# A two-layer hybrid decoder step on one core: squares at the layer seam in PSUM, the decode update of the linear attention ahead of its outputs, and operand sums as a pipeline

## The chip, the cores and the metric

The kernel runs on one core of one Trainium2 chip. The metric is the device time of one execution in microseconds (us), here the median of 3 runs. The core has five engines: TensorE (PE in the profile; PEld is its weight load), VectorE (DVE), ScalarE (ACT), GpSimd (POOL) and SyncE (SP, which issues DMAs). TensorE writes to PSUM, the other memory on the chip is SBUF.

## The reference

One inference step over 1024 prompt rows and 8 decode rows, 1024 channels, two layers. Layer 0 is a gated linear attention of 4 heads beside a short gated convolution; layer 1 a Conformer convolution of width 31; RMS norms stand ahead of each and at the end. Cut to what the change touches:

```
def trunk(x, ...):
    for layer in range(2):
        h = rmsnorm(x, norm_g[layer])           # mean of squares over the 1024 channels
        out = even_layer(h, ...) if layer % 2 == 0 else odd_layer(h, ...)
        x = x + out                             # the seam: x's squares feed the next rmsnorm
    return rmsnorm(x, final_norm_g)

# even_layer, per head; S is (128, 256), one for the prompt and one for each decode row
S_t = diag(a_t) S_{t-1} + k_t^T v_t             # state update
o_t = q_t S_t                                   # output
o   = rmsnorm(o, gla_norm_g) * silu(g)
y   = gate_b * dwconv3(gate_c * hb) * silu(z_b) # projections of h: hb, gate_b, gate_c, z_b
out = concatenate([o, y]) @ w_out
```

All is float32.

## The kernel before

Activations lie transposed: 128 channels on the partitions, 1032 columns (1024 prompt and 8 decode rows) along the free axis, in three blocks of 384, 384 and 264 columns (`CH`). Each product of float32 operands is made of three products of float32r parts: operands are split into a high part (a copy on ACT, `wh`, L240) and a low part (a subtraction, `wl`, L244, on POOL or DVE). A *unit* (L274, called from `units`) is 24 such matmuls, 8 channel tiles by 3 products, for one 128-channel output block and one block of columns, into one of four PSUM buffers of the pool `mmp`. Everything else that needs PSUM takes one of four buffers of the pool `gp` (`g_t`).

All small SBUF tiles come from one ring, `T(...)`, of 25 equal slots: `ring = tc.tile_pool(name="ring", bufs=25)`. A tile keeps its slot until its last reader is done; a new tile waits, with the instruction that writes it, until a slot comes free. The order of ACT's instructions is as written. The order on the other engines is laid down by a planner when the kernel is built, from its own estimates of readiness; at run time every engine works through its queue in order.

Side work is in generators that are called *jobs*: `tick()` runs each started job for one step, and every unit (and every tile of a V projection) ends with a tick. A job that yields n sits out the next n ticks.

Stages in order: V projections (`v_proj`, L351, nine tiles for a head, evacuated by DVE L354); per head the k and q units, `gla(h)` as a job beside `g_proj(h)` (six units) and the next V projection; then sixteen pairs of blocks for the short convolution, of which pairs 3 to 14 are made by a Strassen-like scheme of 7 products (`pair_products`, L728) from sums of operand blocks; the output projection (`x1_add`, L906); the seam (`x1_stat`, `x1_norm`, L884 to L887); layer 1; the final norm.

In `gla(h)` a job step each is: scores (L513); transposes, loads of the decode state and of a, k, q spread over the partitions (`abc`, `kbc`, `qbc`, L538); two steps of state sums (L552, L558); two steps of outputs (L570, L573 on PE, copy L574 on ACT); then the decode state update (POOL multiplies by a, L577; sixteen ACT copies `kv`, L580; POOL adds, L581; store L582); then the decode outputs (POOL product L586, DVE reduction L587), the squares (L590, L591), their sum (L592) and its split (`in_parts`: ACT L397, POOL L398). `OSQ_WAIT` = 4 ticks later the squares are summed over channels on PE (`colsum_parts`, L405), and the norm is applied (L598, L599); 4 ticks after that the result is split (ACT L602, POOL L603) and stored (L605, L606). The gates of the next head (`gates`, L458 to L488, with a scan on DVE, L468) are another job, started `HEAD_AT` = 6, 3, 1 ticks after `gla`.

`build_t` is a job that starts in the first pair, after 6 ticks. It makes the sums of x blocks for the seven products: for each quarter k two loads (L685), two scalings on ACT (L686), four subtractions on DVE (L691 to L694) and three splits (ACT L696, POOL L697). The third pair (q = 2) waits for it before its second block's last units; `pair_sums` (L254 to L257) and `first_pair` (L707, L708) follow there. In the third pair DVE evacuates PSUM at L803 and L801.

At the seam the ring holds the eight x1 tiles, `ss1` and the sixteen tiles of `Bm`, the parts of the short convolution's result that the output projection reads. The sums of the last output block (f = 7) lie in three `gp` buffers. `x1_stat(c)` makes the column sum (L392) and 1/rms; it is written into the middle of a unit of the next block of columns.

Of the kernel before, what the change touches and what calls it, by code (L numbers as in the profile page):

```python
# [7 lines left out]
F32 = mybir.dt.float32  # L8
F32R = mybir.dt.float32r
I32 = mybir.dt.int32  # L10
AF = mybir.ActivationFunctionType
ALU = mybir.AluOpType
# [3 lines left out]
P = 128  # L16
NP = 1024
ND = 8
NT = NP + ND
CH = [(0, 384), (384, 384), (768, 264)]  # L20
KT = 8
# [40 lines left out]
def hybrid_step(ctx, tc, xT, wv, wa, wup, woa, wic, woc, par, ident_d, mask_d, smask_d, sgla, ssc, scc,  # L62
                y_o, glap_o, scp_o, ccp_o, glas_o, scs_o, ccs_o):
    nc = tc.nc
    pe, act, dve, pool, sp = nc.tensor, nc.scalar, nc.vector, nc.gpsimd, nc.sync
# [12 lines left out]
    def nm(s):  # L78
        cnt[0] += 1
        return f"{s}{cnt[0]}"  # L80

    def T(shape, dt=F32, s="t"):
        return ring.tile(shape, dt, tag="t", name=nm(s))
# [4 lines left out]
    def g_t():  # L88
        return gp.tile([P, 512], F32, tag="g", name=nm("g"))
# [16 lines left out]
    def pcol(n, i):  # L106
        return prm[:, PAR[n] + i:PAR[n] + i + 1]
# [260 lines left out]
    vT = {}  # L368
# [133 lines left out]
    def gla(h, V):  # L502
# [33 lines left out]
        for j in (2, 1, 0):  # L536
            t = T([P, ND, P], s="bc")
            sp.dma_start(out=t, in_=dec_d[h, j].partition_broadcast(P))  # L538
            bc.append(t)
        abc, kbc, qbc = bc  # L540
        s0 = [T([P, ND, P], s="s0") for _ in range(2)]
# [5 lines left out]
        for Q in range(2):  # L547
            for jj in range(2):
# [4 lines left out]
                for j in range(2):  # L553
# [3 lines left out]
                    else:  # L557
                        dve.scalar_tensor_tensor(out=sv(p_), in0=sv(p_ - 1), scalar=sm[:, 24 + p_:25 + p_],  # L558
                                                 in1=ps[:, j * DV:(j + 1) * DV], op0=ALU.mult, op1=ALU.add)
            yield  # L560
        sp.dma_start(out=glap_o[h], in_=sv(7))
        o = [T([P, NT], s="o") for _ in range(2)]
        for Q in range(2):
            for hf in range(2):
                ps = g_t()
                hs = slice(hf * P, (hf + 1) * P)
                for j in range(4):
                    p_ = Q * 4 + j
                    lo = Q * 512 + j * P
                    pe.matmul(ps[:, j * P:(j + 1) * P], V[Q][:, j, hs], scT[:, Q, j * P:(j + 1) * P],  # L570
                              start=True, stop=(p_ == 0))
                    if p_ > 0:
                        pe.matmul(ps[:, j * P:(j + 1) * P], sv(p_ - 1)[:, hs], qe[:, lo:lo + P], start=False, stop=True)  # L573
                act.activation(o[hf][:, Q * 512:(Q + 1) * 512], ps, AF.Copy)  # L574
            yield
        for hf in range(2):
            pool.tensor_tensor(out=s0[hf], in0=s0[hf], in1=abc, op=ALU.mult)  # L577
            kv = T([P, ND, P], s="kv")
            for b in range(ND):
                act.activation(kv[:, b, :], kbc[:, b, :], AF.Copy, scale=vT[h][:, hf, b:b + 1])  # L580
            pool.tensor_tensor(out=s0[hf], in0=s0[hf], in1=kv, op=ALU.add)  # L581
            sp.dma_start(out=glas_o[h, hf], in_=s0[hf])  # L582
        yield
        pr = kbc
        for hf in range(2):
            pool.tensor_tensor(out=pr, in0=s0[hf], in1=qbc, op=ALU.mult)  # L586
            dve.tensor_reduce(out=o[hf][:, NP:], in_=pr, axis=mybir.AxisListType.X, op=ALU.add)  # L587
        sq = T([P, NT], s="osq")
        rso = T([P, NT], s="rso")
        act.activation(sq, o[0], AF.Square)  # L590
# [32 lines left out]
    for h in range(H):  # L623
        kq_proj(h)
        start(gla(h, Vs[h]))
        if h + 1 < H:
            start(gates(h + 1), HEAD_AT[h])
        g_proj(h)
        if h + 2 < H:
            Vs.append(v_proj(h + 2))  # L630
# [47 lines left out]
    TQ, T1 = {}, {}  # L678

    def build_t():  # L680
        n = CH[0][1]
        for k in range(4):
            a, b = T([P, 2 * n], s="xa"), T([P, 2 * n], s="xb")
            for t, kk in ((a, k), (b, k + 4)):
                sp.dma_start(out=t, in_=xT[:, kk, 0:2 * n])  # L685
                act.activation(t, t, AF.Copy, scale=pcol("g0", kk))  # L686
            ts = [T([P, 2, n], F32R, s="tq") for _ in range(3)]
            tf = T([P, 2 * n], s="tf")
            f = [tf[:, :n], tf[:, n:], b[:, :n]]
            yield  # L690
            dve.tensor_tensor(out=f[1], in0=b[:, n:], in1=a[:, n:], op=ALU.subtract)  # L691
            dve.tensor_tensor(out=a[:, n:], in0=a[:, n:], in1=a[:, :n], op=ALU.subtract)
            dve.tensor_tensor(out=f[0], in0=b[:, n:], in1=a[:, n:], op=ALU.subtract)
            dve.tensor_tensor(out=f[2], in0=b[:, :n], in1=f[0], op=ALU.subtract)  # L694
            for j in range(3):
                act.activation(ts[j][:, 0, :], f[j], AF.Copy)  # L696
                pool.tensor_tensor(out=ts[j][:, 1, :], in0=f[j], in1=ts[j][:, 0, :].bitcast(F32), op=ALU.subtract)  # L697
            for j in range(3):
                TQ[j + 2, k] = ts[j]
            T1[k] = a[:, n:]  # L700
            yield

    built = build_t()
    start(built, BUILD_AT)
    def first_pair():
# [153 lines left out]
    for lo, n in CH:  # L859
        s = slice(lo, lo + n)  # L860
# [41 lines left out]
    def x1_add(f, c, ps):  # L902
        lo, n = CH[c]
        s = slice(lo, lo + n)
        xt = x1[f]
        dve.tensor_tensor(out=xt[:, s], in0=ps, in1=xt[:, s], op=ALU.add)  # L906
        if f == 0:
            act.activation(ss1[:, s], xt[:, s], AF.Square)
        else:
            sq = g_t() if f < KT - 2 else T([P, 384], s="sq")  # L910
            act.activation(sq[:, :n], xt[:, s], AF.Square)
            dve.tensor_tensor(out=ss1[:, s], in0=sq[:, :n], in1=ss1[:, s], op=ALU.add)

    for f in range(KT - 2):
        x1_tile(f)
        sums = [None] * 3
        if f == 0:
            wy, wo = W("o", f, 1), W("o", f, 0, ahead=1)
            for ks in (slice(0, KT - 1), slice(KT - 1, KT)):
                for c in (0, 2, 1):  # L920
                    sums[c] = unit(c, y_terms(wy, c)[ks], into=sums[c], part=(True, False))
                    tick()
        else:
            wo = W("o", f, 0)
            for c in range(3):
                sums[c] = unit(c, a_terms(wo, O, c), part=(True, False))
                tick()
            wy = W("o", f, 1)
        for c in (0, 2, 1) if f == 0 else range(3):
            x1_add(f, c, unit(c, y_terms(wy, c) if f else a_terms(wo, O, c), into=sums[c]))  # L930
            tick()
        sp.dma_start(out=x1_d[f], in_=x1[f])
# [3 lines left out]
    fs = (KT - 2, KT - 1)  # L936
# [8 lines left out]
    for c, (lo, n) in enumerate(CH):  # L945
        for f in fs:
            if c == 0:
                wy[f] = W("o", f, 1, ahead=1)
            mid = (14, lambda c=c: x1_stat(c - 1)) if c and f == fs[0] else None
            x1_add(f, c, unit(c, y_terms(wy[f], c), mid, into=sums[f, c]))  # L950
            sp.dma_start(out=x1_d[f][:, lo:lo + n], in_=x1[f][:, lo:lo + n])
            if c:
                x1_norm(c - 1, range(4) if f == fs[0] else range(4, KT))
# [114 lines left out]
    for i in range(KT):  # L1068
# [28 lines left out]
        else:  # L1097
            for b, take in ((8 + i, take_gate), (i, take_u)):
                for c, s, ps in units(W("c", b), X):
# [4 lines left out]
                                 in1=pd[:, i, :], op0=ALU.mult, op1=ALU.add)  # L1104
# [237 lines left out]
```

## Time and profile before

| what | us |
|---|---|
| median of 3 runs (lowest, highest) | 1325.4 (1322.89, 1327.21) |
| the profiled execution | 1327.57 |
| its span, first to last instruction | 1325.6 |
| TensorE busy in it | 1272.1 (96%) |
| VectorE busy | 843.4 (64%) |
| GpSimd busy | 679.5 (51%) |
| ScalarE busy | 575.3 (43%) |
| mean granted TensorE clock | 0.976 |

Busy time is the time in which an engine works on an instruction. The granted clock is a share of full speed: 1.00 is 2.4 GHz and 0.50 is 1.2 GHz. The views used below are the list of waits (who stood still, and what ended it), the table by stretches of time, the timeline of one engine, and the chain of work that ended last.

### The profile page before, as it was taken

Reading aid. Unit: us, or ns where it says so; the run is one execution under the profiler, and the core shown is the slowest. Engines: PE = TensorE matmul, PEld = TensorE weight load, DVE = VectorE, ACT = ScalarE, POOL = GpSimd, SP = SyncE. Lnnn points to the kernel's source line nnn. Section 1 sums busy time; section 2 is a strip of 40 time slices with the busy share of each in tenths; the row PEclk is TensorE's granted clock in tenths of the full one; section 3 lists DMA queues with packets and bytes.
Section 4 is the critical chain, followed back from the end, with each engine's and each line's share of the span. In section 5 each row is a group of like instructions: output and inputs, shape, how many; then the busy total and the mean of one; then the engine's idle time right before and its main releaser. Section 6 shows DMA issues by size and latency. Waiting matters only on the chain.

```text
span 1325.6 us, 20388 instructions
## 1 busy us (share of the span) xinstructions
PE 1272.1 (96%) x8189; PEld 1246.6 (94%) x8189; DVE 843.4 (64%) x1145; ACT 575.3 (43%) x890; POOL 679.5 (51%) x410
## 2 busy tenths in 40 slices
PE   8999899999999999999999999998799999998995
PEld 7999799899999889999999999996799999998995
DVE  6542464345526599999985244204569899989636
ACT  7423525425434433332332233313484839548513
POOL 2352653547474674655546232211288888947322
PEclk9999899999999899999999999997899999999898
DMA  7012132133162333233248998722222223223303
GB/s 254 33 64 100 49 128 100 50 135 140 46 225 80 105 127 128 93 115 120 72 151 329 365 379 296 272 114 74 85 98 89 92 90 97 95 96 115 106 20 128
DMA packets 62542, 174.10 MB, mean 131 GB/s; under 512 B 7776, under 2 KB 25792, under 8 KB 62448
## 3 DMA queue, kind: packets, MB, share of 16 engines
q1 hardware_dynamic: 62176, 172.53, 36.8%
q8 instruction: 64, 1.05, 0.3%
q10 hardware_dynamic: 272, 0.27, 0.1%
q14 instruction: 30, 0.25, 0.1%
HBM read 128.37 MB, written 44.41 MB: 130 GB/s over the span
## 4 chain that ended last, share of the span: by engine, by line
PE 85%; DVE 9%; ACT 2%; POOL 2%; issue 1%; DMA 0%; SPq 0%; DVEq 0%; POOLq 0%; ACTq 0%
PE mm L274 59%; PE mm L728 7%; PE g L728 6%; PE mm L351 5%; PE g L274 2%; PE g L552 1%; DVE cv L1151 1%; PE g L513 1%; PE g L570 1%; PE g L392 1%; PE g L573 1%; DVE x L884 1%; PE g L514 1%; DVE Y L1245 1%; DVE tm L468 1%
## 5 line engine op out<-in xcount | busy, mean ns | idle before, releaser
L274 PE MATMUL mm<-A,wh 128*128 128x384 f32 (+1 forms) x1536 | 248.8, 314 | 3.1 <-DVE cs L803 3.1
L274 PEld LDWEIGHTS mm<-A,wh 128*128 128x128 f32 x1536 | 233.8, 189 | 4.3 <-DVE cs L803 3.4
L244 POOL TENSOR_TENSOR wl<-wr,wh 128x1024 fp32r<-128x1024 f32 x51 | 126.1, 2480 | 215.6 <-ACT wh L240 215.6
L274 PE MATMUL mm<-X,wh 128*128 128x384 f32 (+1 forms) x1152 | 200.3, 326 | 5.3 <-ACT X L886 4.9
L274 PEld LDWEIGHTS mm<-X,wh 128*128 128x128 f32 x1152 | 186.3, 191 | 10.1 <-ACT X L886 6.9
L240 ACT ACTIVATE wh<-wr 128x1024 fp32r<-128x1024 f32 (+1 forms) x104 | 108.8, 1054 | 127.4 <-PE g L728 47.0
L274 PE MATMUL mm<-A,wl 128*128 128x384 f32 (+1 forms) x768 | 131.0, 312 | 2.7 <-DVE wl L244 2.7
L274 PEld LDWEIGHTS mm<-A,wl 128*128 128x128 f32 x768 | 118.8, 190 | 3.1 <-DVE wl L244 3.0
L351 PE MATMUL mm<-wh,A 128*128 128x256 f32 (+3 forms) x576 | 111.3, 292 | 6.2 <-ACT A L296 6.2
L1019 POOL TENSOR_TENSOR pa<-pa,pr 128x1024 f32<-128x1024 f32 x45 | 110.4, 2454 | 12.9 <-ACT pr L1017 10.4
L1005 DVE SCALAR_TENSOR_TENSOR g<-u,late,g 128x512 f32<-128x512 f32 x150 | 102.4, 749 | 1.1 <-ACT g L1002 1.1
L274 PE MATMUL mm<-X,wl 128*128 128x384 f32 (+1 forms) x576 | 102.4, 319 | 0.0
L351 PEld LDWEIGHTS mm<-wh,A 128*128 128x128 f32 (+1 forms) x576 | 88.1, 183 | 9.2 <-ACT A L296 6.2
L274 PEld LDWEIGHTS mm<-X,wl 128*128 128x128 f32 x576 | 92.9, 189 | 0.1
L244 POOL TENSOR_TENSOR wl<-s,wh 128x1024 fp32r<-128x1024 f32 x24 | 68.0, 2845 | 39.3 <-ACT wh L240 39.3
L351 PE MATMUL mm<-wl,A 128*128 128x256 f32 (+3 forms) x288 | 84.1, 293 | 0.2
L274 PE MATMUL mm<-M,wh 128*128 128x384 f32 (+1 forms) x384 | 67.5, 328 | 3.3 <-ACT M L1167 2.3
L274 PEld LDWEIGHTS mm<-M,wh 128*128 128x128 f32 x384 | 63.1, 193 | 4.7 <-ACT M L1167 2.6
L978 DVE SCALAR_TENSOR_TENSOR g<-us,prm,g 128x512 f32<-128x512 f32 x70 | 52.9, 755 | 12.5 <-ACT g L976 10.9
L201 ACT ACTIVATE ph<-pw 128x1024 fp32r<-128x1024 f32 x27 | 28.6, 1058 | 68.5 <-DMA pw<-in_dram 38.8
L1017 ACT ACTIVATE pr<-u,late 128x512 f32<-128x512 f32 x90 | 57.2, 717 | 0.0
L274 PE MATMUL mm<-b,wh 128*128 128x384 f32 (+1 forms) x336 | 56.6, 320 | 0.0
(287 smaller groups left out, 2546.3 us busy)
## 6 DMA issues: line engine op xcount, KB each, us to landing
wr<-in_dram SPq DMA_DIRECT2D x102, 512.0 KB, 3.8
pw<-in_dram SPq DMA_DIRECT2D x27, 512.0 KB, 5.6
wl_d<-pw SPq DMA_DIRECT2D x27, 512.0 KB, 5.1
wl<-wl_d SPq DMA_DIRECT2D x27, 512.0 KB, 3.5
b<-y_d SPq DMA_DIRECT2D x14, 516.0 KB, 7.4
bc<-dec_d SPq DMA_DIRECT2D x12, 512.0 KB, 4.9
O<-o_d SPq DMA_DIRECT2D x8, 768.0 KB, 10.4
x<-in_dram SPq DMA_DIRECT2D x8, 516.0 KB, 7.3
```

What stands on the lines that cost most here:

```text
L201: act.activation(h, r, AF.Copy)
L240: act.activation(h[:, :n], raw[:, :n], AF.Copy)
L244: e.tensor_tensor(out=l[:, :n], in0=raw[:, :n], in1=h[:, :n].bitcast(F32), op=ALU.subtract)
L274: pe.matmul(out, wl if p == "w" else wh, xl if p == "x" else xh, start=((first or into is None) and i == 0), stop=(part[1] and i == len(se ...
L351: pe.matmul(ps[:m, :width], x, y[:, ks], start=(i == 0), stop=(i == 23))
L392: pe.matmul(ps[:, :n], ones, t, start=(i == 0), stop=(i == len(terms) - 1))
L468: dve.tensor_tensor_scan(out=b, data0=smask, data1=la, initial=0.0, op0=ALU.mult, op1=ALU.add)
L728: pe.matmul(out, (l if p == "w" else h)[:, ws], xs[k][p == "x"], start=(i == 0), stop=(i == 11))
L978: dve.scalar_tensor_tensor(out=cm if j == 15 else acc, in0=us[:, j:j + n], scalar=ev(j), in1=acc, op0=ALU.mult, op1=ALU.add)
L1005: dve.scalar_tensor_tensor(out=acc[r], in0=u[:, 1 - r, lo + j:hi + j], scalar=df(r, j), in1=acc[r], op0=ALU.mult, op1=ALU.add)
L1017: act.activation(pr[:, r, :], u[:, 1 - r, lo + j:hi + j], AF.Copy, scale=df(r, j))
L1019: pool.tensor_tensor(out=ac, in0=ac, in1=pr, op=ALU.add)
```

## The change

Three edits. In `gla` the decode state update (L576 to L582) moves ahead of the two output steps, and the decode outputs of each half go into the two output steps; the second of these yields 1, so that one tick more passes before the squares. In `build_t` the four quarters run as a pipeline of six one-tick steps: a step loads quarter k + 1, scales and subtracts quarter k and splits quarter k - 1. In `x1_add` the square of the last two output blocks goes to a PSUM buffer, as those of the others do.

```
@@ gla
         sp.dma_start(out=glap_o[h], in_=sv(7))
+        for hf in range(2):
+            kv = T([P, ND, P], s="kv")
+            for b in range(ND):
+                act.activation(kv[:, b, :], kbc[:, b, :], AF.Copy, scale=vT[h][:, hf, b:b + 1])
+            pool.tensor_tensor(out=s0[hf], in0=s0[hf], in1=abc, op=ALU.mult)
+            pool.tensor_tensor(out=s0[hf], in0=s0[hf], in1=kv, op=ALU.add)
+            sp.dma_start(out=glas_o[h, hf], in_=s0[hf])
+        yield
+        pr = kbc
         o = [T([P, NT], s="o") for _ in range(2)]
         for Q in range(2):
             for hf in range(2):
...
                 act.activation(o[hf][:, Q * 512:(Q + 1) * 512], ps, AF.Copy)
-            yield
-        for hf in range(2):
-            pool.tensor_tensor(out=s0[hf], in0=s0[hf], in1=abc, op=ALU.mult)
-            kv = T([P, ND, P], s="kv")
-            for b in range(ND):
-                act.activation(kv[:, b, :], kbc[:, b, :], AF.Copy, scale=vT[h][:, hf, b:b + 1])
-            pool.tensor_tensor(out=s0[hf], in0=s0[hf], in1=kv, op=ALU.add)
-            sp.dma_start(out=glas_o[h, hf], in_=s0[hf])
-        yield
-        pr = kbc
-        for hf in range(2):
-            pool.tensor_tensor(out=pr, in0=s0[hf], in1=qbc, op=ALU.mult)
-            dve.tensor_reduce(out=o[hf][:, NP:], in_=pr, axis=mybir.AxisListType.X, op=ALU.add)
+            pool.tensor_tensor(out=pr, in0=s0[Q], in1=qbc, op=ALU.mult)
+            dve.tensor_reduce(out=o[Q][:, NP:], in_=pr, axis=mybir.AxisListType.X, op=ALU.add)
+            yield Q
@@ build_t
-        for k in range(4):
-            a, b = T([P, 2 * n], s="xa"), T([P, 2 * n], s="xb")
-            for t, kk in ((a, k), (b, k + 4)):
-                sp.dma_start(out=t, in_=xT[:, kk, 0:2 * n])
-                act.activation(t, t, AF.Copy, scale=pcol("g0", kk))
-            ts = [T([P, 2, n], F32R, s="tq") for _ in range(3)]
-            tf = T([P, 2 * n], s="tf")
...
-            yield
-            dve.tensor_tensor(out=f[1], in0=b[:, n:], in1=a[:, n:], op=ALU.subtract)
...
+        xs, fs = [], []
+        for step in range(6):
+            if step < 4:
+                xs.append([T([P, 2 * n], s="xa") for _ in range(2)])
+                for t, k in zip(xs[step], (step, step + 4)):
+                    sp.dma_start(out=t, in_=xT[:, k, 0:2 * n])
+            if 0 < step < 5:
+                k = step - 1
+                a, b = xs[k]
+                for t, kk in ((a, k), (b, k + 4)):
+                    act.activation(t, t, AF.Copy, scale=pcol("g0", kk))
+                tf = T([P, 2 * n], s="tf")
+                f = [tf[:, :n], tf[:, n:], b[:, :n]]
+                dve.tensor_tensor(out=f[1], in0=b[:, n:], in1=a[:, n:], op=ALU.subtract)
...
+            if step > 1:
+                k = step - 2
+                for j in range(3):
+                    t = TQ[j + 2, k] = T([P, 2, n], F32R, s="tq")
+                    act.activation(t[:, 0, :], fs[k][j], AF.Copy)
+                    pool.tensor_tensor(out=t[:, 1, :], in0=fs[k][j], in1=t[:, 0, :].bitcast(F32), op=ALU.subtract)
             yield
@@ x1_add
-            sq = g_t() if f < KT - 2 else T([P, 384], s="sq")
+            sq = g_t()
```

## Rows read from the trace of the kernel before

**Rows 1.** The page, busy us of each engine, share of the span, instructions.

```profile
PE 1272.1 (96%) x8189; PEld 1246.6 (94%) x8189; DVE 843.4 (64%) x1145; ACT 575.3 (43%) x890; POOL 679.5 (51%) x410
```

**Rows 2.** PE's waits, who <- what ended it: us in total, times, longest.

```profile
PE g L392 <- DVE ss L912: 8.6, 2, 7.6
PE g L405 <- ACT sh L397: 8.0, 2, 5.4
...
PE mm L274 <- DVE cs L803: 3.1, 1, 3.1
PE mm L274 <- DVE wl L244: 2.7, 1, 2.7
```

**Rows 3.** Stretches: length, busy (instructions) PE PEld DVE ACT POOL, clock, DMA share, GB/s.

```profile
155.33:162.16 6.83, 5.19 (x23) 3.52 (x24) 1.82 (x5) 1.06 (x1) 5.07 (x2) 0.50 0.00 0
250.91:254.32 3.41, 2.93 (x12) 2.11 (x13) 0.66 (x2) 1.71 (x2) 2.38 (x1) 0.50 0.00 0
445.47:452.29 6.82, 6.13 (x19) 6.13 (x20) 3.27 (x6) 3.66 (x6) 3.96 (x4) 0.50 0.40 132
469.36:472.77 3.41, 3.30 (x13) 3.31 (x14) 3.41 (x3) 1.06 (x1) 3.41 (x2) 0.50 0.63 155
907.15:936.16 29.01, 15.13 (x57) 10.88 (x55) 21.78 (x38) 17.09 (x32) 8.62 (x9) 0.66 0.23 73
936.16:940.40 4.24, 4.24 (x15) 4.14 (x14) 2.54 (x7) 1.65 (x5) 0.00 (x0) 0.50 0.52 185
```

**Rows 4.** Stretches, the same columns, of layer 1's projections.

```profile
940.00:1175.00 235.00, 235.00 (x1504) 234.87 (x1504) 201.18 (x296) 144.94 (x230) 180.98 (x117) 1.00 0.29 95
```

**Rows 5.** Chain that ended last, at the seam: start us, us, what.

```profile
911.22 0.93 PE g L392 x2
...
935.48 1.25 PE g L392 x2
```

**Rows 6.** Timeline, ACT, seam: start, us, what, count [idle before <- what ended it].

```profile
908.44 0.53 ACT L911 ACTIVATE sq<-x 128x384 f32<-128x384 f32 x1 [32.00 <-PE g L274]
...
933.20 1.99 ACT L240 ACTIVATE wh<-wr 128x1024 fp32r<-128x1024 f32 x2
```

**Rows 7.** Timeline, ACT, heads 0 and 1.

```profile
120.14 0.60 ACT L574 ACTIVATE o<-g 128x512 f32<-128x512 f32 x1 [10.86 <-PE g L573]
...
130.57 4.79 ACT L580 ACTIVATE kv<-bc,vT 128x128 f32<-128x128 f32 x16
...
155.85 1.06 ACT L397 ACTIVATE sh<-osq 128x1032 fp32r<-128x1032 f32 x1 [2.31 <-DVE osq L592]
...
250.28 1.06 ACT L397 ACTIVATE sh<-osq 128x1032 fp32r<-128x1032 f32 x1 [1.30 <-DVE osq L592]
```

**Rows 8.** Timeline, DVE, heads 0 and 1, the scan of the next head's gates.

```profile
142.88 4.39 DVE L468 TENSOR_TENSOR_SCAN tm<-smask,la 128x1032 f32<-128x1032 f32 x1
...
221.93 2.31 DVE L468 TENSOR_TENSOR_SCAN tm<-smask,la 128x1032 f32<-128x1032 f32 x1
```

**Rows 9.** Timeline, POOL, heads 0 and 1.

```profile
141.78 3.33 POOL L586 TENSOR_TENSOR bc<-s,bc 128x1024 f32<-128x1024 f32 x1 [1.49 <-DVE o L587]
...
235.69 4.79 POOL L581 TENSOR_TENSOR s<-s,kv 128x1024 f32<-128x1024 f32 x2
```

**Rows 10.** Timeline, DVE, third pair.

```profile
445.55 1.35 DVE L803 TENSOR_TENSOR cs<-mm,rs 128x384 f32<-128x384 f32 x3
...
460.55 1.50 DVE L254 TENSOR_TENSOR s<-wr 128x512 f32<-128x512 f32 x1 [2.07 <-POOL tq L697]
```

**Rows 11.** Timeline, ACT, third pair.

```profile
435.42 0.94 ACT L696 ACTIVATE tq<-tf 128x384 fp32r<-128x384 f32 x2 [5.46 <-DVE tf L693]
...
436.68 2.00 ACT L602 ACTIVATE sg<-o 128x1032 fp32r<-128x1032 f32 x2
```

**Rows 12.** Timeline, SP's queue, third pair: the load of the last quarter.

```profile
442.78 0.42 SPq L685 DMA_DIRECT2D xa<-in_dram  x1
```

**Rows 13.** Line L691, its instructions: ns least/median/most, first and last start us.

```profile
L691 DVE TENSOR_TENSOR tf<-xb,xa x4: 549/980/2327, 417.3 to 453.9; 128x384 f32<-128x384 f32 x4
```

More of the change, by code (lines that the diff above doesn't have):

```diff
@@ L681, in build_t @@
         n = CH[0][1]
-        for k in range(4):
-            a, b = T([P, 2 * n], s="xa"), T([P, 2 * n], s="xb")
-            for t, kk in ((a, k), (b, k + 4)):
-                sp.dma_start(out=t, in_=xT[:, kk, 0:2 * n])
-                act.activation(t, t, AF.Copy, scale=pcol("g0", kk))
-            ts = [T([P, 2, n], F32R, s="tq") for _ in range(3)]
-            tf = T([P, 2 * n], s="tf")
-            f = [tf[:, :n], tf[:, n:], b[:, :n]]
-            yield
-            dve.tensor_tensor(out=f[1], in0=b[:, n:], in1=a[:, n:], op=ALU.subtract)
[L692 to L700, printed above, removed]
+        xs, fs = [], []
@@ new lines, in build_t @@
+        for step in range(6):
[11 more added lines that the diff above has]
+                dve.tensor_tensor(out=f[1], in0=b[:, n:], in1=a[:, n:], op=ALU.subtract)
+                dve.tensor_tensor(out=a[:, n:], in0=a[:, n:], in1=a[:, :n], op=ALU.subtract)
+                dve.tensor_tensor(out=f[0], in0=b[:, n:], in1=a[:, n:], op=ALU.subtract)
+                dve.tensor_tensor(out=f[2], in0=b[:, :n], in1=f[0], op=ALU.subtract)
+                T1[k] = a[:, n:]
+                fs.append(f)
+            if step > 1:
[4 more added lines that the diff above has]
+                    pool.tensor_tensor(out=t[:, 1, :], in0=fs[k][j], in1=t[:, 0, :].bitcast(F32), op=ALU.subtract)
```

## The prediction

> **What bounds the kernel now.** I read the page first: TensorE (PE) is busy 1272.1 us of the 1325.6 us span, and its idle time is a few per cent [rows 1]. So no other engine's busy time is worth anything in itself; only the places count where PE stands still. The list of PE's waits gives them by name [rows 2]: the column sum of the new x at the seam (L392, 8.6 us, two places), the column sum of a head's squares (L405, 8.0 us in two places), and two waits of 3.1 and 2.7 us in the third pair of projection blocks. The table by stretches shows what comes on top [rows 3]: after each stop the granted clock is 0.50, that is 1.2 instead of 2.4 GHz, for 3.4 to 6.8 us, and work done there takes twice its time. Between them PE is busy without a break (940 to 1175 us: 235.00 of 235.00, at clock 1.00) [rows 4], so time won ahead of such a stretch stays won. From that row a matmul takes 235.00/1504 = 0.156 us at full clock, on a mean of 344 columns; a unit of 24 takes 4.2 us with 384 columns and 2.9 us with 264.
>
> What each stop costs, idle time plus half the busy time at clock 0.50 behind it [rows 2, 3]: head 0: 5.4 + 5.19/2 = 8.0. Head 1: 8.0 - 5.4 = 2.6, + 2.93/2 = 4.0. Third pair: 3.1 + 6.13/2 = 6.1, and 2.7 + 3.30/2 = 4.4. Seam: the 29.01 us from 907.15 hold one unit of 264 (2.9), one of 384 (4.2) and three column sums (0.9 each [rows 5]), 9.8 us of work; 19.2 are lost, and 4.24/2 = 2.1 behind them: 21.3. Together 43.8 us. That is the most these edits can give.
>
> **The seam (L910).** The last two output blocks f = 6, 7 put the square in a ring tile (L910), the others in PSUM. The ring has 25 slots: eight x1, ss1 and the sixteen Bm tiles are 25. A square can only get the slot of a Bm tile, and PE reads those until its last unit. The trace shows just this: ACT sits 32.00 us ahead of the first square and PE ends the wait, at 908.44 [rows 6]. The change takes the square from the four-buffer PSUM pool; three of these are the sums of f = 7 and one is free, and each sum is freed as it is used. The cost of the instruction itself is nil: same size, same engines.
>
> The first block of columns is done on PE two units of 384 and two of 264 before 907.15 + 2.9, at 895.9; an add, a square (0.53 [rows 6]) and an add more, and the column sum can start at 898 instead of 911.22: 13.2 us earlier. What follows runs on ACT and DVE in order, in rounds: from the first sum to the third it took 935.48 - 911.22 = 24.3 us, 12.1 a round [rows 5]. Behind the second round stand the weights of the second gate unit (L240 at 933.20 [rows 6]), and PE takes that unit up at 936.16 [rows 3]. Two bounds. If all of it just moves, PE is there at 936.16 - 13.2 = 923.0. If PE never waits, at 936.16 - 19.2 = 917.0. The second block's columns exist at 904.2, so the second round can start between 906 (at once) and 910 (a full round later), and the unit with it between 919 and 923. I take 921: 15.2 us, and the 2.1 us of slow clock: **17 us**, with 10 (shifted, slow clock again, and two short stops) and 21 as ends.
>
> **Heads (gla).** The generator steps once per tick, and a tick is one unit on PE. The state update moves from tick 7 to tick 5, the outputs from 5 and 6 to 6 and 7, with the product and reduction in the same ticks; the `yield Q` adds one idle tick, so the squares go from tick 8 to 9 and the column sum L405 from 13 to 14. No instruction is added or removed. Moved with the update: sixteen ACT copies, POOL's two multiplications and two additions, two stores on SP's queue.
>
> Head 0: the sixteen copies (4.79 us) now stand between the outputs and the next head's gates [rows 7]. At tick 5 ACT is idle anyway, 10.86 us ahead of the output copies [rows 7]; that hides them. If that cover is gone they cost 4.8 us of ACT, not of PE, since PE only needs the squares. The gates then start some 4 us earlier; their scan takes 2.31 us in head 1 but 4.39 in head 0 [rows 8], where the update's product ran on POOL beside it [rows 9], another 2.1. The split square, done at 156.9 [rows 7], would be done near 150.8; PE is there at 151.5 (156.9 - 5.4). The wait goes; I take **7** of 8.0 (ends 4 and 8), as the DVE evacuations that queue behind the square's sum may hold PE a little.
>
> Head 1: gates come first (tick 4), so the copies (here too 4.8 us) now stand ahead of the output copies and the silu. POOL is what is late: its state additions start at 235.69 behind the gates' products [rows 9] and hardly move; the split square comes perhaps 1.3 us earlier than 251.3 [rows 7]. The extra tick (2.9 us) may give PE other work or may not, since on PE the planner, not the code, had already put L405 behind the eighth V tile. The two kv tiles also hold ring slots while V of head 3 asks for two. I take **2.5** of 4.0 (ends -2 and 4). SP's queue: the state stores, and any load behind them, wait on POOL's additions as before, only earlier. Heads 2 and 3 have no stop at L405 and give nothing; head 3's normalization starts one unit (4.2 us) later, into the pipeline below.
>
> **Operand sums (build_t).** Before, each of four quarters was load, scale (ACT), four subtractions (DVE), split (ACT, POOL), two ticks each: ACT waits for DVE's sums (5.46 us before L696) and DVE for ACT's next scaling, each in order, and the third pair's first evacuation L803 comes only at 445.55 behind them [rows 10, 11]. PE, with four buffers, stops at 443.1. The pipeline scales quarter k while it splits k-1 and loads k+1, in six ticks instead of eight. That breaks the to-and-fro; the last split leaves earlier, so that L254, which waits for it (2.07 us) at 460.55 [rows 10], and the weights behind it, come earlier too. Against it: the same DVE work falls into fewer ticks, beside head 3's, and ring slots. At the last split the pipeline holds 4 sums, 12 parts and 2 sources, head 3 four (o, SG), the first pair three, rs and rs2 two: 27, before the third pair's cs and ch. So the last parts wait for head 3's stores: L602 at 436.68, a slot at 442.78, 6.1 us [rows 11, 12]. PE's four buffers cover 15.5 us. I take **6** of 10.5 (ends -4 and 10.5).
>
> **What the Trainium skill would say.** L691, one and the same shape, takes between 0.55 and 2.33 us [rows 13]; one product on POOL lengthens a scan on DVE [rows 8, 9]. The Trainium skill, "SBUF — State Buffer", section "Who interferes with whom", has it that a DVE instruction with two SBUF inputs and a GpSimd instruction that reads SBUF exclude each other for a whole instruction. By that rule the pipeline, which sets POOL's splits of one quarter beside DVE's sums of the next, would be a loss, the first rival below.
>
> **The sum.** 17 + 7 + 2.5 + 6 = 32.5 us. The profiled execution took 1327.6 us, 2.0 of it around the span of 1325.6; the median of the runs is 1325.4, 2.2 lower, and the same 32.5 come off it: **1293**, with 1285 to 1302 if all four hold roughly.
>
> **The rivals.**
> 1. DVE and POOL collide in the pipeline. Sixteen subtractions at up to 2.33 instead of 0.55 us [rows 13] are up to 28 us more; beyond the 15.5 us of PE's buffers some 12 come out on PE, as a loss in place of the gain of 6: 1325.4 - 32.5 + 18 = 1311. For it: the row. Against: POOL ran beside these sums before as well. 0.13.
> 2. The seam's gain is cut by half because ACT and DVE, not the ring, set the pace there: the third round ends late, PE stops at the third block of columns too, and the clock falls again: seam 8 instead of 17, 1302. For it: DVE is busy 21.78 of 29.01 us there [rows 3]. 0.15.
> 3. All stops go: 1325.4 - 43.8 = 1282. 0.08.
> 4. Slower: the ring jams in the third pair. cs waits for a slot that only head 3's stores free, DVE stands at L803, PE stops after four units. It decides the sign only if it costs PE more than the 26.5 us of the other parts. The longest slot wait here is ACT's 32.00 [rows 6]; taken whole, it gives 1325.4 - 26.5 + 32 = 1331. 0.04.
> 5. The squares don't get out (the fourth PSUM buffer is not free when asked for): 1325.4 - 15.5 = 1310. 0.03.
>
> **How the numbers follow.** The forecast, 1293, has 0.57. Cases 1, 2, 3 and 5 are all faster. Within 0.3% (4 us, about what a measurement of this kernel can tell from no change) takes rival 1 with a poor seam: 0.03. Slower: 0.04. Faster: 0.93. The range runs from rival 3 to rival 1: 1281 to 1312.
>
> **What the profile after would show.** Seam: the first square near 892 instead of 908, L392 three times inside or right behind PE's units, PE at the second gate unit by 917 to 923, clock 1.00. Head 0: sixteen copies inside ACT's idle stretch before the outputs, scan at 2.3, no wait at L405. Third pair: L803 within four units of its matmuls, no wait for wl. I am wrong if PE's waits name DVE or ACT at the seam for more than 8 us in all, if the subtractions exceed 2 us each, or if a new wait shows on L803 or on V of head 3.

## The result, and the profile after

| | before | after |
|---|---|---|
| median, us | 1324.1 | 1302.1 |
| lowest and highest, us | 1322.22, 1327.21 | 1301.01, 1304.05 |
| profiled execution, us | 1327.57 | 1301.23 |
| its span, us | 1325.6 | 1299.5 |
| mean granted TensorE clock | 0.976 | 0.988 |

The ratio is 0.9833, with a 95% interval of 0.9808 to 0.9858: 22.0 us off the median, where 32.5 were forecast. The time, 1302.1, lies inside the range (1281 to 1312) and 9.1 us above the forecast of 1293.0; the narrower 1285 to 1302, given for the case that all four parts hold roughly, was just missed. Executions of before differ among themselves: beside e9, one took 1327.79 us at a mean granted clock of 0.976 and one 1322.25 at 0.983, so the profiled one stands at the upper end.

The page, busy us of each engine (after; it answers to [rows 1]):

```profile
PE 1258.1 (97%) x8189; PEld 1238.2 (95%) x8189; DVE 808.6 (62%) x1145; ACT 575.9 (44%) x890; POOL 674.3 (52%) x410
```

PE's waits, who <- what ended it: total, times, longest (after; against [rows 2]):

```profile
PE g L392 <- DVE ss L917: 8.2, 1, 8.2
...
PE g L733 <- ACT wh L240: 4.8, 1, 4.8
...
PE g L405 <- ACT sh L397: 1.0, 1, 1.0
```

The table by stretches (after; columns as in [rows 3]): the place of head 0's old stop, the slow clock in the third pair and at the seam, and the quiet stretch behind them.

```profile
155.33:162.16 6.83, 6.83 (x41) 6.56 (x41) 4.56 (x11) 5.84 (x12) 0.96 (x1) 1.00 0.01 2
...
435.85:442.68 6.83, 5.35 (x17) 5.35 (x18) 5.37 (x6) 4.72 (x5) 6.22 (x5) 0.50 0.25 90
...
906.89:913.72 6.83, 3.32 (x10) 3.12 (x11) 5.20 (x9) 4.37 (x8) 2.56 (x3) 0.50 0.42 148
920.00:1175.00 255.00, 255.00 (x1620) 253.66 (x1619) 219.46 (x310) 155.22 (x245) 197.59 (x129) 1.00 0.28 92
```

Head 0 has no stop left and head 1 has 1.0 us, at full clock. The third pair keeps one stop of 4.8 us, the seam one of 8.2, and behind both the granted clock is still 0.50.

To see where time went I compared the end of the same matmul (the n-th on PE) in the two profiled executions. After is 0.4 us behind at the start, gains 8.1 us at head 0, 2.9 at head 1, 3.8 in the third pair and 11.3 at the seam, and is 25.8 us ahead behind it. The stops account for it, each counted as in the prediction (idle plus half the busy time at clock 0.50): head 0 8.0 to 0, head 1 4.0 to 1.0, third pair 10.5 to 4.8 + 5.35/2 = 7.5, seam 21.3 to 0.4 + 8.2 + 3.32/2 = 10.3.

The seam, timeline of after (start, us, what [idle before <- what ended it]; `g` on ACT and DVE is the square, now in PSUM):

```profile
877.82 0.50 ACT L916 ACTIVATE g<-x 128x384 f32<-128x384 f32 x1 [15.92 <-DVE x L911]
...
882.56 0.56 DVE L917 TENSOR_TENSOR ss<-g,ss 128x384 f32<-128x384 f32 x1 [0.56 <-ACT g L916]
...
886.68 0.81 PE L392 MATMUL g<-ss,ones 128*128 128x384 f32 x2
...
890.50 0.56 DVE L911 TENSOR_TENSOR x<-g,x 128x384 f32<-128x384 f32 x1
...
892.74 1.58 ACT L891 ACTIVATE X<-x 128x384 fp32r<-128x384 f32 x3
...
894.22 0.48 ACT L916 ACTIVATE g<-x 128x384 f32<-128x384 f32 x1
...
898.30 0.55 DVE L917 TENSOR_TENSOR ss<-g,ss 128x384 f32<-128x384 f32 x1
...
898.90 0.91 PE L392 MATMUL g<-ss,ones 128*128 128x384 f32 x2
...
908.11 1.99 ACT L240 ACTIVATE wh<-wr 128x1024 fp32r<-128x1024 f32 x2
...
909.93 0.42 DVE L917 TENSOR_TENSOR ss<-g,ss 128x264 f32<-128x264 f32 x1
...
910.40 1.25 PE L392 MATMUL g<-ss,ones 128*128 128x264 f32 x2 [8.20 <-DVE ss L917]
...
911.07 3.15 PE L274 MATMUL mm<-X,wh 128*128 128x384 f32 x9
```

The squares do get out: the first is done as soon as its sum exists, where before it sat 32.00 us [rows 6]. PE is 14.5 us ahead when it gets here, so 911.22 and 936.16 of before [rows 3, 5] would be 896.7 and 921.7 in this clock. The first column sum runs at 886.68, 10.0 us earlier; the second gate unit at 911.07, 10.6 us earlier. From sum to sum it takes 12.2 and 11.5 us, as before (12.1 on the mean). The reader can see why: the last square of the second block has its x at 891.1, but stands on ACT behind three instructions of the norm (L891) until 894.22, and its sum on DVE behind the norm's work until 898.30. The third round goes the same way, and the third column sum stands on PE's queue ahead of the second gate unit.

The heads, ACT, DVE and POOL of after (the copies `kv`; head 0's scan and split square; head 1's state additions and split square):

```profile
111.92 4.80 ACT L565 ACTIVATE kv<-bc,vT 128x128 f32<-128x128 f32 x16 [2.29 <-DMA bc<-dec_d]
...
149.59 1.07 ACT L397 ACTIVATE sh<-osq 128x1032 fp32r<-128x1032 f32 x1 [2.42 <-DVE osq L591]
```

```profile
139.39 2.31 DVE L468 TENSOR_TENSOR_SCAN tm<-smask,la 128x1032 f32<-128x1032 f32 x1
```

```profile
225.32 4.81 POOL L567 TENSOR_TENSOR s<-s,kv 128x1024 f32<-128x1024 f32 x2
```

```profile
240.93 1.06 ACT L397 ACTIVATE sh<-osq 128x1032 fp32r<-128x1032 f32 x1 [1.30 <-DVE osq L591]
```

The copies run in ACT's idle time ahead of the outputs, the scan has gone from 4.39 to 2.31 us [rows 8], and the split square from 155.85 to 149.59 [rows 7]. In head 1 POOL's additions start 10.4 us earlier than in [rows 9], of which 8 come from head 0; the split square gains 9.35.

The third pair, timeline of after:

```profile
431.60 0.51 ACT L704 ACTIVATE tq<-tf 128x384 fp32r<-128x384 f32 x1
...
433.60 0.52 ACT L704 ACTIVATE tq<-tf 128x384 fp32r<-128x384 f32 x1 [1.49 <-DMA o_d<-sg]
...
435.81 0.52 ACT L704 ACTIVATE tq<-xa 128x384 fp32r<-128x384 f32 x1 [1.69 <-POOL o L602]
436.24 1.04 ACT L240 ACTIVATE wh<-wr 128x1024 fp32r<-128x1024 f32 x1
...
437.31 1.46 DVE L244 TENSOR_TENSOR wl<-wr,wh 128x1024 fp32r<-128x1024 f32 x1 [7.08 <-ACT wh L240]
...
437.33 2.93 PE L733 MATMUL g<-A,wh 128*128 128x384 f32 x8 [4.81 <-ACT wh L240]
...
438.69 1.35 DVE L808 TENSOR_TENSOR cs<-mm,rs 128x384 f32<-128x384 f32 x3
439.96 2.72 DVE L254 TENSOR_TENSOR s<-wr 128x512 f32<-128x512 f32 x1
```

This is the jam the prediction described, smaller and through another door: the last split of the operand sums (L704) waits for head 3's store and for its product on POOL; behind it on ACT are the weights of the next pair, the first by the scheme of seven products (L240), and PE waits for those at that pair's first product (L733). The first evacuation (L808) stands on DVE behind the low part of the same weights, so PE's four buffers were full as well: it had made four units, from 416.91 to 432.5 us. The planner has put this product ahead of the unit that stood in its place on PE in before, but that unit too would have had to wait for L808. The two old stops are gone, and L254, at 439.96, comes at 450.6 in before's clock (PE is 10.6 us ahead here), where it came at 460.55 [rows 10].

### The profile page after: what moved, and what is told of

It is laid out like the page before. It is cut to its first block, busy times and chain, and to the rows that moved or that the text cites. A ratio compares the mean times of both kernels' runs of the same rounds, so it can differ in the third digit from the quotient of the medians.

```text
span 1299.5 us, 20371 instructions
## 1 busy us (share of the span) xinstructions
PE 1258.1 (97%) x8189; PEld 1238.2 (95%) x8189; DVE 808.6 (62%) x1145; ACT 575.9 (44%) x890; POOL 674.3 (52%) x410
## 4 chain that ended last, share of the span: by engine, by line
PE 87%; DVE 6%; POOL 3%; ACT 2%; issue 2%; DMA 0%; SPq 0%; DVEq 0%; POOLq 0%; ACTq 0%
PE mm L274 60%; PE mm L733 8%; PE mm L351 6%; PE g L733 6%; PE g L274 1%; PE g L552 1%; DVE cv L1156 1%; PE g L513 1%; POOL tq L705 1%; PE g L579 1%; PE g L582 1%; PE g L392 1%; DVE x L889 1%; PE g L514 1%; DVE Y L1250 1%
## 5 line engine op out<-in xcount | busy, mean ns | idle before, releaser
L274 PE MATMUL mm<-A,wh 128*128 128x384 f32 (+1 forms) x1536 | 246.2, 311 | 0.0
L244 POOL TENSOR_TENSOR wl<-wr,wh 128x1024 fp32r<-128x1024 f32 x51 | 125.1, 2460 | 194.3 <-ACT wh L240 179.1
L274 PE MATMUL mm<-X,wh 128*128 128x384 f32 (+1 forms) x1152 | 195.2, 321 | 0.4 <-DVE X L892 0.4
L274 PEld LDWEIGHTS mm<-X,wh 128*128 128x128 f32 x1152 | 183.7, 189 | 2.5 <-DVE X L892 1.2
L240 ACT ACTIVATE wh<-wr 128x1024 fp32r<-128x1024 f32 (+1 forms) x104 | 109.0, 1055 | 145.2 <-PE g L733 66.2
L1024 POOL TENSOR_TENSOR pa<-pa,pr 128x1024 f32<-128x1024 f32 x45 | 110.4, 2454 | 12.8 <-ACT pr L1022 10.4
L244 POOL TENSOR_TENSOR wl<-s,wh 128x1024 fp32r<-128x1024 f32 x24 | 65.6, 2744 | 40.7 <-ACT wh L240 40.7
```

The lines of the kernel that those rows point to most:

```text
L240: act.activation(h[:, :n], raw[:, :n], AF.Copy)
L244: e.tensor_tensor(out=l[:, :n], in0=raw[:, :n], in1=h[:, :n].bitcast(F32), op=ALU.subtract)
L274: pe.matmul(out, wl if p == "w" else wh, xl if p == "x" else xh, start=((first or into is None) and i == 0), stop=(part[1] and i == len(se ...
L1024: pool.tensor_tensor(out=ac, in0=ac, in1=pr, op=ALU.add)
```

## The experiments

Gains on the chip are given as ratios to before; 0.01 is 13.2 us. "Progress" is the lead on PE at the same matmul over the profiled execution of before.

**One edit at a time.** e1_seam is before with the last hunk alone, e2_heads with the hunk of `gla` alone, e3_sums with that of `build_t` alone.

```
e1:  -            sq = g_t() if f < KT - 2 else T([P, 384], s="sq")
     +            sq = g_t()
e2:  the hunk "@@ gla" of the change and nothing else
e3:  the hunk "@@ build_t" of the change and nothing else
```

> The kernel before with the seam's edit alone (squares of the last two blocks to PSUM). If the 25 slots of the ring were what held the first square at 908.4 us, it starts some 16 us earlier here, and the second gate unit starts 10 to 11 us earlier than at 936.2, as in the changed kernel: about 1313 us. If the seam's gain there came from the other two edits, which also free PE ahead of it, this stays at 1322 to 1325.

> The kernel before with the decode update moved, alone. If the stops of heads 0 and 1 at L405 came from the copies and products of the update that stood ahead of the squares, both go: 8 and 3 us, about 1313 us; and the third pair keeps its two stops (3.1 and 2.7 us) or gets longer ones, since head 3's stores come one unit later. If the update only trades places with other work, less than 4 us.

> The kernel before with the pipelined operand sums, alone. One theory: the wait for ring slots at the last split comes from head 3's stores being one tick late; here they are a tick earlier, the stop of 4.8 us shrinks to under 2, and this gives 6 to 10 us: 1314 to 1318. The other: the pipeline itself asks for more slots than there are, whenever head 3 stores; then the stop stays at 4 to 5 us and this gives 3 to 4 us: about 1320.

| kernel | median, us | ratio to before [95%] | gain by the ratio, us |
|---|---|---|---|
| e1_seam | 1315.0 | 0.9933 [0.9912, 0.9954] | 8.9 |
| e2_heads | 1312.4 | 0.9911 [0.9893, 0.9929] | 11.8 |
| e3_sums | 1323.6 | 0.9993 [0.9983, 1.0004] | 0.9 |
| after | 1302.1 | 0.9833 [0.9808, 0.9858] | 22.1 |

The single gains sum to 21.6 us: the three edits add up, within intervals of 1.4 to 2.8 us to either side for the single gains. In e1 progress at the seam grows by 11.1 us and PE's wait at L392 is 8.2 us, exactly as in after, so the shortfall at the seam has nothing to do with the other two edits. In e2 the stops of the heads go (0.96 us is left) and progress grows by 11.0 us there, and by 3.0 more in the third pair. There its two stops become four of 0.9 to 1.7 us, which was not expected; PE stands still as long as before (5.9 us in all, 5.8 before), but the clock stays at 1.00, where before's profile has 10.2 us at 0.50. So this gain is one of the clock. Why the clock held I didn't separate.

e3 shows what the pipeline does when the heads stand as before. PE's waits and the timeline of e3:

```profile
PE g L734 <- ACT wh L240: 6.3, 1, 6.3
```

```profile
437.34 5.35 POOL L603 TENSOR_TENSOR o<-o,sg 128x1032 f32<-128x1032 f32 x2
...
440.51 2.60 DVE L697 TENSOR_TENSOR tf<-xa,xa 128x384 f32<-128x384 f32 x1
...
443.19 0.94 ACT L705 ACTIVATE tq<-tf 128x384 fp32r<-128x384 f32 x2 [2.57 <-DVE tf L697]
```

The two stops of 3.1 and 2.7 us [rows 2] have become one of 6.3 us: the same weights as in after, late behind the last splits, which here wait among others for subtractions of 2.6 us beside POOL's work for head 3. The median moves by 0.9 us with an interval around zero, less than either theory had (1314 to 1318, about 1320). In its profile progress in the third pair still grows by 3.1 us, though PE stands still longer than before: the clock is at 0.50 for 6.8 us there instead of 10.2.

**The extra tick.** e4_tick is after without it.

```
-            yield Q
+            yield
```

> The changed kernel without the extra tick after the outputs (yield in place of yield Q): squares, column sum and store of each head come one unit earlier. If the moved update alone removes the stop of head 0, there is still none; head 1's stop of 1.0 us stays or grows to 2; and head 3's stores, one unit earlier, take 2 to 4 us off the third pair's stop: 1299 to 1302. If the tick is what removes the stops, head 0 waits 2 us or more at L405 again: 1304 to 1308.

1302.6 us (ratio 0.9835 [0.9817, 0.9852]), the same as after; PE has no stop at head 0, 0.96 us at head 1, 4.3 in the third pair and 8.2 at the seam. The tick does nothing to the time; the moved update alone takes the stops away. The 2 to 4 us that were expected off the third pair's stop did not come (4.8 to 4.3).

**The seam's next limits.** In e5_norm all of a block's norm stands behind both adds and squares of the next block; e6_weights leaves the norm as in after, splits the next unit's weights early and puts the third column sum into the second gate unit.

```
e5:  -            if c:
     -                x1_norm(c - 1, range(4) if f == fs[0] else range(4, KT))
     +            if c and f == fs[1]:
     +                x1_norm(c - 1)
e6, in x1_add:
     +            if c == 2 and f == fs[0]:
     +                split_ahead(len(parts) + 1)
e6, ahead of the first gate units:
     -                for w, take in zip(ws, (take_gate, take_u)):
     -                    mid = (14, lambda: x1_stat(2)) if c == 0 and take is take_gate else None
     ...
     +                ps = [unit(c, a_terms(ws[0], X, c))]
     +                ps.append(unit(c, a_terms(ws[1], X, c), None if c else (14, lambda: x1_stat(2))))
     +                if c == 0:
     +                    x1_norm(2)
     +                take_gate(c, ps[0])
     +                take_u(c, ps[1])
```

> The changed kernel with the seam's norms of a block of columns behind both of the next block's squares, so that on ACT and DVE no square waits behind a norm it doesn't need. If the rounds of 12 us at the seam come from that order, the second column sum starts 4 to 6 us earlier, the third no longer holds PE for 8 us, and the second gate unit starts about 5 us earlier: about 1297. If the arithmetic of a round itself (ACT, DVE) sets the pace, the rounds stay at 11 to 12 us and the time within 2 us of 1302.

> The changed kernel with the weights of the second gate unit split ahead of the second block's norm, and the third column sum moved behind that unit on PE. If PE's 8.2 us there are an order on its own queue (a sum that isn't ready ahead of a unit that could be), the second unit follows the first at once, 8 to 9 us earlier, the wait moves to the third sum and shrinks to 3 to 4 us: 1296 to 1298. If the norms of the second block bound PE anyway, the wait only moves: within 2 us of 1302.

e5: 1299.4 us (0.9811 [0.979, 0.9832]). From sum to sum it now takes 9.2 and 5.9 us instead of 12.2 and 11.5. The third column sum no longer waits, but the second gate unit does, and starts 3.4 us earlier where about 5 were expected (timeline of e5):

```profile
895.69 0.81 PE L392 MATMUL g<-ss,ones 128*128 128x384 f32 x2
...
901.59 0.60 PE L392 MATMUL g<-ss,ones 128*128 128x264 f32 x2
...
906.55 1.99 ACT L240 ACTIVATE wh<-wr 128x1024 fp32r<-128x1024 f32 x2
...
907.65 4.81 PE L274 MATMUL mm<-X,wh 128*128 128x384 f32 x14 [5.46 <-ACT wh L240]
```

The weights stand on ACT behind the eight instructions of the norm: 8.2 us of wait turn into 5.5. e6: 1297.2 us (0.9794 [0.9776, 0.9812]). Here the second gate unit starts at 901.89 with a wait of 0.45 us, and the wait moves one block on, to a sigmoid, where the third sum was expected (PE's waits of e6):

```profile
PE mm L274 <- ACT sig L1082: 4.2, 1, 4.2
```

A sigmoid that frees PSUM stands behind the third block's norm on ACT. Each cure so far uncovers the next instruction in ACT's written order. So the seam was held by order on ACT and on DVE, not by the ring any more. The times of e5, e6 and e7 are each a few us under after's with intervals that overlap it; what they show, they show in the traces.

**Slots in the third pair.** e7_slots is after with two ring slots less in the operand sums (four results in two tiles, so that the scaled sources can go earlier).

```
+                if k % 2 == 0:
+                    t1 = T([P, 2, n], s="t1")
+                T1[k] = t1[:, k % 2, :]
-                dve.tensor_tensor(out=a[:, n:], in0=a[:, n:], in1=a[:, :n], op=ALU.subtract)
+                dve.tensor_tensor(out=T1[k], in0=a[:, n:], in1=a[:, :n], op=ALU.subtract)
```

> The changed kernel with the four sums T1 in two ring tiles instead of in the four load tiles: two slots less, the same instructions. If the stop of 4.8 us in the third pair (and the slow clock behind it, 2.7) comes from the last splits that wait for slots of head 3's stores, it shrinks to under 1.5 us: 1295 to 1297. If it comes from POOL's and DVE's load there, it stays: 1301 to 1303.

1298.6 us (0.9806 [0.9788, 0.9824]), between the two theories; the stop goes from 4.8 to 2.5 us. So slots were about half of it.

**All three together.** e8_all is after with e5, e6 and e7.

> The three last edits together on the changed kernel. If seam and third pair are separate stops, the gains add up: 8 to 10 us at the seam, 5 to 7 in the third pair, 1285 to 1290. If the seam's two edits are two ways to the same few us and the norm of the third block bounds what is left, 1292 to 1295.

1289.1 us (0.9734 [0.9716, 0.9752]): 35 us faster than before and 13 than after, with e10 the fastest kernel here with the whole computation. By themselves e5, e6 and e7 give 2.7, 4.9 and 3.5 us, 11.1 in sum. With the norm behind the adds the sigmoid's wait is 1.7 instead of 4.2 us, and the clock stays at 1.00 in both places. At the seam progress over before is 19.6 us here, where it was 11.3 in after and 21.3 were counted as lost.

**What is left in the third pair.** e9_nopool is e8 with POOL's twelve low parts made by ACT copies; the low parts are left out of the computation. e10_build4 is e8 with the operand sums started after 4 ticks.

```
e9:  -  pool.tensor_tensor(out=t[:, 1, :], in0=fs[k][j], in1=t[:, 0, :].bitcast(F32), op=ALU.subtract)
     +  act.activation(t[:, 1, :], fs[k][j], AF.Copy)
e10: -  STAGE_AT, BUILD_AT = (6, 5), 6
     +  STAGE_AT, BUILD_AT = (6, 5), 4
```

> The kernel of e8_all, but the twelve low parts of the operand sums are made by ACT copies in place of POOL's subtractions, so that POOL does not read beside DVE there (the low parts are left out of the computation: they hold the rounded high part again). ACT gets 12 x 0.5 = 6 us of work more. Theory 1 (what is left of the third pair's stop, 2.54 us in e8_all, comes from DVE's subtractions being lengthened beside POOL's splits): subtractions of 0.55 to 0.7 us instead of 1.25 to 2.83, ACT waits no longer for them, the stop is under 0.7 us, no slow clock there; about 1286.5 us against 1289.1 of e8_all. Theory 2 (the subtractions are long for another reason, or the stop comes from the order on ACT): they stay above 1.2 us or ACT's six microseconds more push the weights back; the stop stays at 2.5 or grows; 1289 to 1293 us.

> The kernel of e8_all with the job of the operand sums started 4 ticks into the first pair instead of 6, some 8 us earlier. Theory 1 (the last splits are late because the sums start late; PE's four buffers would hide the rest): all splits, and with them the weights of the third pair, come up to 8 us earlier; stop of 2.54 us gone; 1286 to 1287 us. Theory 2 (ring slots decide: the sums then meet more of head 3's tiles and wait for its stores, which stand where they stood): ACT and DVE wait for slots in the middle of the sums, and the stop stays between 2 and 5 us; 1289 to 1292 us.

e9: 1285.6 us (0.971 [0.9691, 0.9728]). The sixteen subtractions, groups (busy us, mean ns | idle before), first before, then after, then the two longest of e8, then e9:

```profile
L692 DVE TENSOR_TENSOR xa<-xa 128x384 f32<-128x384 f32 x4 | 4.9, 1228 | 0.1
L691 DVE TENSOR_TENSOR tf<-xb,xa 128x384 f32<-128x384 f32 x4 | 4.8, 1209 | 5.4 <-ACT xb L686 5.4
L693 DVE TENSOR_TENSOR tf<-xb,xa 128x384 f32<-128x384 f32 x4 | 4.3, 1076 | 0.1
...
L694 DVE TENSOR_TENSOR xb<-xb,tf 128x384 f32<-128x384 f32 x4 | 2.2, 558 | 0.2
```

```profile
L695 DVE TENSOR_TENSOR xa<-xa 128x384 f32<-128x384 f32 x4 | 5.0, 1248 | 0.1
...
L694 DVE TENSOR_TENSOR tf<-xa,xa 128x384 f32<-128x384 f32 x4 | 3.7, 936 | 0.6 <-ACT xa L691 0.6
L696 DVE TENSOR_TENSOR tf<-xa,xa 128x384 f32<-128x384 f32 x4 | 3.6, 898 | 0.1
L697 DVE TENSOR_TENSOR xa<-xa,tf 128x384 f32<-128x384 f32 x4 | 3.4, 858 | 0.1
```

```profile
L697 DVE TENSOR_TENSOR tf<-xa,xa 128x384 f32<-128x384 f32 x4 | 5.9, 1466 | 1.5 <-ACT xa L691 1.5
...
L700 DVE TENSOR_TENSOR xa<-xa,tf 128x384 f32<-128x384 f32 x4 | 4.9, 1247 | 0.1
```

```profile
L697 DVE TENSOR_TENSOR tf<-xa,xa 128x384 f32<-128x384 f32 x4 | 3.5, 874 | 2.2 <-ACT xa L691 2.2
...
L699 DVE TENSOR_TENSOR tf<-xa,t 128x384 f32<-128x384 f32 x4 | 2.2, 552 | 0.0
L698 DVE TENSOR_TENSOR t<-xa 128x384 f32<-128x384 f32 x4 | 2.2, 549 | 0.4 <-ACT xa L691 0.4
L700 DVE TENSOR_TENSOR xa<-xa,tf 128x384 f32<-128x384 f32 x4 | 2.1, 554 | 0.1
```

In e8 the last split waits for such a subtraction, and the weights stand right behind it (timeline of e8):

```profile
432.61 0.52 ACT L706 ACTIVATE tq<-xa 128x384 fp32r<-128x384 f32 x1 [1.74 <-DVE xa L700]
```

That subtraction took 2.64 us beside head 3's product on POOL (L602); the longest of e8, 2.83 us, stood beside the low part of weights (L244). Without POOL's splits three of the four take 0.55 us, the sums are done before that product starts, and PE has no stop in the third pair at all, although ACT has twelve copies more. The first theory holds in the trace; the time, 3.2 us less by the ratios where 2.6 were expected, has intervals that overlap. What was left of the stop was DVE's subtractions lengthened beside POOL, by the splits and by its other work. The groups also say that before paid the same (16.2 us in sum) as after (15.7): the change neither brought nor cured this.

e10: 1288.9 us (0.9735 [0.9713, 0.9756]), the same as e8. The weights come earlier and the stop at the product is gone, but PE stops 2.1 us at an evacuation (`zs`, L820) that now stands on DVE behind the sums. Neither theory foresaw that: the wait moved, and nothing was won.

## Why the prediction was right, and where it was wrong

The direction, the named places and the range (31 us wide) held; the sum, 32.5, was 10.5 us over the 22.0 measured (the forecast itself missed by 1.3 less, as before's median is now 1324.1 and was 1325.4). By its own steps:

| term | forecast, us | progress, before to after | by itself on the chip |
|---|---|---|---|
| seam | 17 (10 to 21) | 11.3 | 8.9 (e1) |
| head 0 | 7 (4 to 8) | 8.1 | with head 1: |
| head 1 | 2.5 (-2 to 4) | 2.9 | 11.8 (e2), third pair included |
| operand sums | 6 (-4 to 10.5) | 3.8 | 0.9 (e3) |
| sum | 32.5 | 26.1 | 21.6 |

**Seam: right mechanism, wrong size.** The step that failed is "the second round can start between 906 (at once) and 910 (a full round later)". In before's clock the second column sum came at 898.90 + 14.5 = 913.4 and the third at 924.9, and PE took up the second gate unit at 925.6, where 919 to 923 had been worked out. By itself the edit is worth 8.9 us, under the low end of 10. Two things in it: the first sum was ready when forecast (883.1, that is 897.6), but ran at 886.68, seven matmuls into PE's next unit; and the rounds did not overlap at all, since the last square of each block and its sum stand behind the norm of the block before on ACT and DVE. This is rival 2 (ACT and DVE set the pace), whose seam of 8 us was nearer than the forecast's 17, though its total of 1302, the measured time, is luck in part: the heads gave more and the sums less than it took for them. The row that the prediction held for it, DVE busy 21.78 of 29.01 us [rows 3], was the one to believe; e5, e6 and e8 show that the order on these two queues, and no missing slot, was the limit; with another order the same stage gives 19.6 us. The prediction's own test said so as well: more than 8 us of PE's waits at the seam name DVE (8.2), and the clock, forecast at 1.00, was 0.50 for 6.83 us.

**Heads: right.** Copies in ACT's idle time, the scan at 2.3 us, no wait at L405; the split square, done at 150.7, was forecast "near 150.8". e4 settles what the prediction left open: the extra tick gives nothing. In head 1 the split square came 1.3 us earlier than head 0's gain explains (9.35 less 8.1), as forecast.

**Operand sums: mis-sized.** The to-and-fro was broken, L254 did come earlier, by 10 us, and both old stops went. What failed is the step "PE's four buffers cover 15.5 us", by which the wait for head 3's stores was to cost PE little. PE used its four buffers up (15.6 us) and then stood still for 4.8 us more: on ACT the weights of the next pair, and through them on DVE the first evacuation, stood behind the split that waited for head 3. The prediction had named the wait (27 slots asked of 25, head 3's stores) but not what stands behind it on these two queues. By itself the edit is worth 0.9 us (0 within its interval), not 6. The 3.8 us of progress in the table are not its own: e2 without it shows 3.0 there and e3 with it alone 3.1, both with less slow clock and not with less standing still, and e1, where nothing in this place is changed, shows 1.2. So the mechanism of rival 4 was there, at 4.8 us of stop and not at 32, and it was the last split that waited for the slot, not cs. e7 shows that slots were about half of it, e9 that the rest is DVE beside POOL.

**Rival 1 (DVE and POOL collide): the row is right, the sign is not.** Subtractions of up to 2.65 us stand in after, over the limit of 2 that the prediction set itself, but before has the same (2.63). The Trainium skill, "SBUF — State Buffer", section "Who interferes with whom", says that a DVE instruction with two SBUF inputs contends with a GpSimd instruction that reads SBUF; e9 agrees (0.55 us in three of four groups without POOL's splits; in e8 up to 2.83, beside POOL's low part of weights). By that rule alone the pipeline would have been a loss; it wasn't, as POOL worked beside the old order just as much (16.2 us of subtractions before, 15.7 after).

**Profile against median.** The two profiled spans differ by 26.1 us, the medians by 22.0. The prediction took its prices from one execution that was 3.4 us above its median. The share of the clock in it can be seen: behind head 1's stop of 2.6 us the clock was 0.50 for 3.41 us in it [rows 3], and 1.00 in e1, where this code and this stop (2.57 us) are the same (table by stretches, e1):

```profile
250.91:254.32 3.41, 3.27 (x27) 2.63 (x28) 0.32 (x1) 1.37 (x2) 2.42 (x1) 1.00 0.00 0
```

In e3's profile too, PE is 2.6 us ahead of before's by the end of head 1 (0.4 of it from the start), with nothing changed up to there. And in the third pair, unchanged in e1, the same two stops (3.1 and 2.7 us) had 3.4 us of slow clock behind them in e1 and 10.2 in before's profile. The slow clock behind a short stop is thus a price that an execution pays or does not, and the full 1.5 us that I counted for it belonged to that execution.

## What to carry to other kernels

When a missing buffer is cured, the work that waited for it falls back on the order in which its engines' queues were written, so price the cure by walking that order instruction by instruction: here, where DVE was busy for three quarters of the stage, the cure gave 11 of the 21 us that PE lost, and 20 once the order was changed too. Count what stands behind a jam on every engine's queue, weights for PE and evacuations among it, before spare PSUM buffers are set against it. A price taken from one execution should be set beside the median before it goes into a sum.

## What the runs showed of the hardware that was not expected

The same stop does not always bring the slow clock. PE's stop of 2.54 us at the product behind the third pair's units (L735) is the same in e7 and e8, at the same matmul; the stretch from 436 us on, of e7 and then of e8:

```profile
436.00:440.00 4.00, 4.00 (x15) 3.40 (x14) 4.00 (x6) 2.15 (x3) 4.00 (x5) 0.58 0.37 134
```

```profile
436.00:440.00 4.00, 3.40 (x18) 3.08 (x19) 4.00 (x5) 1.40 (x2) 4.00 (x5) 1.00 0.27 96
```

The stop of 1.0 us in head 1 of after had no slow clock behind it; the stops of 4.2 us and more in these places (4.2 in e6, 4.8 and 8.2 in after, 6.3 in e3) all had it. How long the clock stays slow was not fixed either: behind head 0's stop of 5.4 us, the same in before, e1 and e3, the clock was 0.50 for 6.8 us in the first two and for 3.4 us in e3.
